# Where stores are queued and how long a side matmul waits: out-projection and up stage of a hybrid decoder layer

## The chip, the cores and the metric

One core of a Trainium2 chip runs the whole layer. The metric is the device time of one execution in microseconds (us). TensorE (PE) does the matmuls, ScalarE (ACT) and VectorE (DVE) the elementwise work, GpSimd (POOL) a few fills and many transfers, SyncE (SP) only transfers. SP, ACT and POOL each have one queue in which they start transfers (DMAs), and each of them works through its instructions in order.

## The reference, cut to what matters

x is 2048 tokens by 1024 channels, float32, one layer.

```
h   = RMSNorm(x); z = h @ w_in
mix = concat(attention(z), conv_module(z), rg_lru(z))
x   = x + mix @ w_out                       # out-projection
ff  = square(relu(RMSNorm(x) @ w_up))       # up stage, 4096 wide
x   = x + ff @ w_down                       # down stage
out = RMSNorm(x)
```

The attention is a dilated window attention with three patterns; the conv module has 31 taps, a LayerNorm (two totals over channels) and a swish; rg_lru has a 4-tap convolution, two gates by small matmuls, and a scan.

## The kernel before, in words

Channels lie on the 128 partitions and tokens along the free axis. The tokens go in two halves h of 1024. Every float32 operand is split into a rounded part and a rest (`split` L233, `halves` L887: a cast on ACT, then a subtraction on DVE), and each product is three matmuls, 128x128 by 512 columns.

The stages on PE, in order: in-projection of half 0 and of half 1, with the three mixers of half 0 beside the latter; then, for each half, out-projection, up stage, down stage. The mixers of half 1 run beside the out-projection, up and down stage of half 0.

**The mixers of half 1** are a generator, `mixers(1)`, that yields a cost after each step. The main stages call `tick(share)` (L858) at fixed places: a tick adds the share to a credit that is held under two shares, takes one step of the generator when the credit is positive, and subtracts the step's cost. A tick's PE, DVE and ACT instructions are placed behind the main ones traced so far. There are two ticks in each of the 56 groups of 24 matmuls of the down stage (L1486), seven for each of the 16 passes of the up stage and two for each out-projection tile. `yield 0` costs nothing, so it only puts the next step at the next tick. What is left of the mixers when the down stage of half 0 reaches its last product is traced at once (L1551 to L1554). The mixers of half 0 are run through without ticks, so that a yield changes nothing there. In `conv_norm` (L467) and `lru_mixer` (L522) a split is followed by a yield and then by the matmuls that read it (L275, L276; L549 to L551).

**The out-projection** (`outproj`, L993) makes 16 tiles of 128 channels by 512 tokens, tile n in the order of `ORDER` (L893): first the later 512 tokens of the half (n 0 to 7, m = 1), then the earlier (n 8 to 15, m = 0). A tile is 24 matmuls into one of four banks. Its weights, 512 KB, are loaded by `out_load` (L911) two or three tiles ahead into a buffer that an earlier tile has read, and split by `out_split`. The old x (`residual`, L1008) is loaded into `e_at`, a ring of three tiles for half 0 and of four for half 1; DVE adds the bank (L1069). `evac` (L1012) scales a copy g on ACT (L1015), stores e to `xscr` (L1016), adds the square to a sum, splits g, and makes the sums S1, S2, S3 of the 2x2 block scheme that the up stage multiplies by. It stores g to `ascr` where m = 1 (L1024), and S2 to `ascr` for tiles 8 to 11 (L1037), once two subtractions and two splits are done. These stores are POOL's, where they share the queue with the attention's loads. `in_order` (L1045) holds SP's transfers in the order in which the tile loop traces them; the other order is the scheduler's, which places instructions by when its own model has them ready.

**The up stage** (`up`, L1097) has 16 passes f of seven products with 12 matmuls each. Weights are loaded on SP (L959 to L961, L976) into buffers that the splits of the pass before free. The results are squared (L1119, L1120), summed on DVE (L1177, L1192, L1199) and stored to `fscr` by `put` (L1114), seven stores a pass on ACT's queue. The result tiles are a ring of six. The down stage (`down`, L1331) loads them again on SP.

Of the kernel before, what the change touches and what calls it, by code (L numbers as in the profile page):

```python
# [77 lines left out]
def body(tc, xt, w_in, w_v, w_out, w_up, w_down, vecs, lru_wa, lru_wx, consts, out):  # L78
    nc = tc.nc
# [50 lines left out]
    def work(h):  # L130
        return wide_tile() if h == 0 else mtile()
# [16 lines left out]
    def conv_bank():  # L148
        return pc.tile([P, NB], F32, name="cb", tag="cb")
# [17 lines left out]
    xscr = tc.dram_tile([KT, P, S], F32, name="xscr")  # L167
    nscr = tc.dram_tile([2, HS], F32, name="nscr")
    fscr = tc.dram_tile([2, 7, NSET, P, NB], F32, name="fscr")
    ascr = tc.dram_tile([3, KH, P, NB], F32, name="ascr")  # L170
# [296 lines left out]
    def conv_norm(t0, yc, early):  # L467
        tile_, q = wide_tile if early else mtile, nc.sync if early else nc.gpsimd
        s = tile_()[:, :NB]
        nc.vector.tensor_add(s, yc[0], yc[1])  # L470
        pair = work_pair(0 if early else 1)
        split(s, *pair)
        yield 1.4
        bank = conv_bank()
        total(bank, ones_cr, pair)
        yield 0
        for a in yc:
            nc.vector.tensor_sub(a, a, bank)
        q0 = tile_()[:, :NB]
        nc.scalar.activation(s, yc[0], AF.Square)  # L480
        nc.scalar.activation(q0, yc[1], AF.Square)
        yield 1.4
        nc.vector.tensor_add(q0, q0, s)
        pair = work_pair(0 if early else 1)
        split(q0, *pair)
        yield 1.4
        bank = conv_bank()
        total(bank, ones_cr, pair)
        yield 0
        nc.scalar.activation(s, bank, AF.Sqrt, bias=eps_l)  # L490
        nc.vector.reciprocal(s, s)
        yield 3.3
        for t, a in enumerate(yc):
            nc.vector.tensor_mul(a, a, s)
            nc.scalar.activation(a, a, AF.Silu, scale=v("conv_ln_g", t), bias=v("conv_ln_b", t))
        yield 1.4
        for t, a in enumerate(yc):
            q.dma_start(mscr[3 + t][:, t0:t0 + NB], a)
        yield 0
# [22 lines left out]
    def lru_mixer(h):  # L522
        n = HS if h == 0 else NB
        for t0 in range(h * HS, (h + 1) * HS, n):
            for t in range(3):
                x = work(h)
                gw = mtile_r() if h else early_gates
                loads(h).dma_start(x[:, :n + 3], lscr[t][:, t0 + 29:t0 + n + 32])
                loads(h).dma_start(gw.bitcast(F32), gates_w[t])
                u = work(h)[:, :n]  # L530
                if h:
                    yield 0
                    yield 0
                nc.vector.tensor_scalar(u, x[:, 0:n], v("lru_conv_w", t * LTAPS), v("lru_conv_b", t), op0=OP.mult, op1=OP.add)
                for k in range(1, LTAPS):
                    if k == 2:
                        yield 1.3
                    nc.vector.scalar_tensor_tensor(u, x[:, k:k + n], v("lru_conv_w", t * LTAPS + k), u, op0=OP.mult, op1=OP.add)
                yield 1.5
                r, i = work(h)[:, :n], work(h)[:, :n]  # L540
                for c in range(0, n, NB):
                    uh, ul = work_pair(h)
                    split(u[:, c:c + NB], uh, ul)
                    yield 0.7
                    for m, (dst, name) in enumerate(((r, "lru_ba"), (i, "lru_bx"))):
                        bank = mix_bank() if h and m else conv_bank()
                        wh, wl = (gw[:, part * P:(part + 1) * P] for part in (m, 2 + m))
                        with first():
                            nc.tensor.matmul(bank, wh, uh, start=True, stop=False)  # L549
                            nc.tensor.matmul(bank, wh, ul, start=False, stop=False)  # L550
                            nc.tensor.matmul(bank, wl, uh, start=False, stop=True)  # L551
                        nc.scalar.activation(dst[:, c:c + NB], bank, AF.Sigmoid, bias=v(name, t))
                    yield 0
                nc.vector.tensor_mul(u, u, i)
                gg = work(h)[:, :n]
                loads(h).dma_start(gg, gscr[t][:, t0:t0 + n])
                a = work(h)[:, :n]
                nc.scalar.activation(a, r, AF.Exp, scale=splus[:, 12 + t:13 + t])
                nc.scalar.activation(r, r, AF.Tanh, scale=splus[:, 9 + t:10 + t])
                yield 0.7  # L560
                nc.scalar.activation(i, a, AF.Square)
                nc.vector.scalar_tensor_tensor(r, i, 1.0, r, op0=OP.add, op1=OP.mult)
                nc.scalar.activation(r, r, AF.Sqrt)
                yield 0.7
                nc.vector.tensor_mul(u, u, r)
                init = 0.0 if t0 == 0 else state[:, t:t + 1]
                nc.vector.tensor_tensor_scan(i, a, u, init, OP.mult, OP.add)
                if t0 + n < S:
                    nc.vector.tensor_copy(state[:, t:t + 1], i[:, n - 1:n])
                yield 2.1  # L570
                nc.vector.tensor_mul(gg, gg, i)
                yield 0.7
                stores(h).dma_start(mscr[5 + t][:, t0:t0 + n], gg)
# [337 lines left out]
    def out_load(n, pairs):  # L911
        nc.sync.dma_start(f32(out_pair(n, pairs)[1]), out_w[ORDER[n][1]])
# [80 lines left out]
    def outproj(h, wts, banks, begun):  # L993
        at, pairs = wts.at, wts.pairs
# [17 lines left out]
        def evac(n):  # L1012
            m, d, tok = where(n)
            e, g = e_at[n % es], scaled[n % 4]
            nc.scalar.activation(g, e, AF.Copy, scale=v("norm2_g", d))  # L1015
            nc.gpsimd.dma_start(xscr[d][:, tok], e)  # L1016
            if n % 8 == 0:
                nc.scalar.activation(sq[m], e, AF.Square)
            else:
                nc.scalar.activation(sqt, e, AF.Square)  # L1020
                nc.vector.tensor_add(sq[m], sq[m], sqt)
            k = d % 4
            if m == 1:
                nc.gpsimd.dma_start(ascr[d // 4, k], g)  # L1024
            if m == 1 and d >= 4:
                split_op(A22, k, g)
                s1 = held.pop(k)
                nc.vector.tensor_add(s1, s1, g)
                split_op(S1, k, s1)
            elif m == 0 and d < 4:  # L1030
                s3, s2 = back.pop(k)
                split_op(A11, k, g)
                nc.vector.tensor_sub(s3, g, s3)
                split_op(S3, k, s3)
                nc.vector.tensor_sub(s2, s2, s3)
                split_op(S2, k, s2)
                nc.gpsimd.dma_start(ascr[2, k], s2)  # L1037
            else:
                held[k] = g

# [15 lines left out]
        for n in range(16):  # L1056
            if 1 <= n < 4:
                act_load(h, 0, *((2, 4), (4, 5), (5, 8))[n - 1])
            if n >= begun:
                out_matmuls(n, pairs, banks, range(4))  # L1060
                tick(OUT_SHARE)
                out_matmuls(n, pairs, banks, range(4, KT))
            if n + 1 < 16 and n + 1 > begun - 1:
                out_split(n + 1, pairs)
            if 1 <= n <= 4:
                act_split(0, 2 * n - 2)
                act_split(0, 2 * n - 1)
            with first():
                nc.vector.tensor_add(e_at[n % es], e_at[n % es], banks[n % 4])  # L1069
            evac(n)  # L1070
            if 4 <= n + 3 < 8:
                out_load(n + 3, pairs)
            if 8 <= n + 2 < 16:
                out_load(n + 2, pairs)
            if 7 <= n <= 10:
                back[n - 7] = s_at(), s_at()
                nc.sync.dma_start(back[n - 7][0], ascr[0, n - 7])
                nc.sync.dma_start(back[n - 7][1], ascr[1, n - 7])
            if n + 2 < 16:
                residual(n + 2)  # L1080
            if n == 12:
                wts.load(0)
            elif n == 13:
                wts.sums(0)
                wts.first()
            elif n == 14:
                wts.second()
            in_order()
            tick(OUT_SHARE)
# [7 lines left out]
    def up(h, wts, banks, rest, prologue):  # L1097
# [14 lines left out]
                nc.tensor.matmul(bank, wl[:, sl], hi(x), start=False, stop=k == KH - 1, **kw)  # L1112

        def put(q, f, t):  # L1114
            nc.scalar.dma_start(fscr[h, q, f], t)

        def squared(t, src):
            with first():
# [34 lines left out]
        for f in range(NSET + 1):  # L1153
# [8 lines left out]
            if f < NSET:  # L1162
                d = d_[f % 2]
# [357 lines left out]
    pairs = []  # L1521
# [18 lines left out]
    for h in range(2):  # L1540
        wraw, plain, at, more = low_tiles(h)
        pairs = pairs + more
# [38 lines left out]
        else:  # L1581
            pairs = state_["pairs"]
# [53 lines left out]
```

## Time and profile before

| | us |
|---|---|
| three runs | 2063.57, 2066.7, 2083.01 |
| median | 2066.7 |
| profiled execution | 2067.54 |
| its span, first to last instruction | 2065.7 |
| PE busy in the span | 1979.6 |
| DVE, ACT, POOL busy | 1500.4, 1054.6, 198.7 |

The span is what the trace covers; the execution's own time is 1.8 us longer. An engine's busy time counts its work and not the time in which it starts transfers or waits. A share of the clock below 1 in a stretch says that TensorE ran part of it at the lower of its two levels (1.2 instead of 2.4 GHz).

### The profile page before, as it was taken

The numbers are of one execution on the slowest core, as the hardware profiler recorded it, in microseconds if no ns is written. First come the engines' busy times: TensorE is split into PE (matmuls) and PEld (weight loads), VectorE is DVE, ScalarE is ACT, GpSimd is POOL, SyncE is SP. The second block draws the span as 40 slices with busy tenths as digits, with TensorE's granted clock in tenths as the row PEclk, the third lists the DMA queues.
The fourth block names the chain that finished last, engine by engine and source line by source line (L and its number), as shares of the span: only waits on it lengthen the run. The fifth ranks groups of instructions, "written<-read, shape, count | busy, mean of one in ns | idle before, by whom it ended". The sixth has DMA issues, their size and how long they took to land.

```text
span 2065.7 us, 25592 instructions
## 1 busy us (share of the span) xinstructions
PE 1979.6 (96%) x8876; PEld 1593.9 (77%) x8876; DVE 1500.4 (73%) x2009; ACT 1054.6 (51%) x1623; POOL 198.7 (10%) x352
## 2 busy tenths in 40 slices
PE   8999999999889999999999999999999999999997
PEld 6877777887667777888777778877888887778885
DVE  7898865587667665888888996777555555697855
ACT  6144974333557754465656554356455455344341
POOL 0113100000233413000000000120000000000000
PEclk9999999999999999999999999999999999999999
DMA  5555684734786648445976684685444448876834
GB/s 172 171 147 156 181 293 145 254 118 134 227 249 174 199 141 252 151 169 183 357 264 237 207 286 157 216 280 192 152 153 149 151 149 290 307 264 215 271 106 143
DMA packets 205165, 416.31 MB, mean 202 GB/s; under 512 B 26118, under 2 KB 34550, under 8 KB 204972
## 3 DMA queue, kind: packets, MB, share of 16 engines
q1 hardware_dynamic: 148884, 284.86, 42.1%
q0 software_dynamic: 20688, 60.59, 9.5%
q10 hardware_dynamic: 35464, 69.23, 9.0%
q8 instruction: 70, 1.15, 0.2%
q14 instruction: 59, 0.48, 0.1%
HBM read 299.79 MB, written 123.19 MB: 205 GB/s over the span
## 4 chain that ended last, share of the span: by engine, by line
PE 66%; DMA 12%; DVE 11%; issue 6%; ACT 4%; POOL 1%; SPq 1%; DVEq 0%; ACTq 0%; POOLq 0%
PE bank L1110 9%; PE bank L1111 9%; PE bank L1112 9%; PE bank L1425 6%; PE bank L1424 6%; PE bank L1426 6%; DMA rounded<-fscr 4%; PE mm L255 3%; PE mm L258 3%; PE mm L261 3%; DMA pair<-out_w 3%; DVE rounded L889 2%; DVE wide L462 2%; PE bank L926 1%; PE bank L924 1%
## 5 line engine op out<-in xcount | busy, mean ns | idle before, releaser
L1110 PE MATMUL bank<-rounded,pair 128*128 128x512 f32 x896 | 355.2, 396 | 3.5 <-ACT low L1208 3.0
L1111 PE MATMUL bank<-rounded,pair 128*128 128x512 f32 x896 | 353.0, 394 | 0.0
L1112 PE MATMUL bank<-rounded,pair 128*128 128x512 f32 x896 | 352.0, 393 | 0.0
L888 ACT CAST rounded<-rounded 128x1024 fp32r<-128x1024 f32 (+1 forms) x168 | 160.3, 967 | 310.2 <-DMA rounded<-fscr 220.8
L889 DVE TENSOR_TENSOR rounded<-rounded 128x1024 fp32r<-128x1024 f32 (+1 forms) x168 | 185.9, 1117 | 130.3 <-ACT rounded L888 130.1
L1425 PE MATMUL bank<-rounded,rounded 128*128 128x512 f32 x672 | 263.5, 392 | 7.0 <-DVE rounded L889 7.0
L1424 PE MATMUL bank<-rounded,rounded 128*128 128x512 f32 x672 | 263.9, 393 | 5.5 <-DVE z L1437 3.8
L1426 PE MATMUL bank<-rounded,rounded 128*128 128x512 f32 x672 | 262.7, 391 | 0.0
L1110 PEld LDWEIGHTS bank<-rounded,pair 128*128 128x128 f32 x896 | 168.6, 188 | 44.2 <-ACT low L1208 3.4
L1112 PEld LDWEIGHTS bank<-rounded,pair 128*128 128x128 f32 x896 | 168.7, 188 | 37.2 <-issue 0.4
L1111 PEld LDWEIGHTS bank<-rounded,pair 128*128 128x128 f32 x896 | 168.8, 188 | 35.9 <-issue 0.5
L255 PE MATMUL mm<-rounded,rounded 128*128 128x512 f32 x496 | 160.1, 399 | 9.3 <-ACT rounded L235 7.6
L261 PE MATMUL mm<-rounded,rounded 128*128 128x512 f32 x496 | 158.5, 394 | 0.0
L258 PE MATMUL mm<-rounded,rounded 128*128 128x512 f32 x496 | 158.0, 396 | 0.0
L1424 PEld LDWEIGHTS bank<-rounded,rounded 128*128 128x128 f32 x672 | 126.7, 189 | 36.5 <-issue 5.8
L1425 PEld LDWEIGHTS bank<-rounded,rounded 128*128 128x128 f32 x672 | 126.6, 188 | 36.1 <-DVE rounded L889 9.7
L1426 PEld LDWEIGHTS bank<-rounded,rounded 128*128 128x128 f32 x672 | 126.7, 189 | 26.4
L235 ACT CAST rounded<-raw 128x512 fp32r<-128x512 f32 (+1 forms) x96 | 55.7, 583 | 158.8 <-PE mm L258 105.3
L888 ACT CAST pair<-wraw 128x1024 fp32r<-128x1024 f32 x64 | 67.2, 1051 | 115.0 <-PE bank L1111 85.9
L889 DVE TENSOR_TENSOR rounded<-block,rounded 128x1024 fp32r<-128x1024 f32 x96 | 116.3, 1217 | 6.3 <-ACT rounded L888 6.3
L889 DVE TENSOR_TENSOR pair<-wraw,pair 128x1024 fp32r<-128x1024 f32 x64 | 78.2, 1221 | 58.6 <-ACT pair L888 58.6
L255 PEld LDWEIGHTS mm<-rounded,rounded 128*128 128x128 f32 x496 | 93.4, 190 | 31.5 <-ACT rounded L235 7.9
(325 smaller groups left out, 3816.7 us busy)
## 6 DMA issues: line engine op xcount, KB each, us to landing
block<-in_w_down SPq DMA_DIRECT2D x128, 512.0 KB, 5.4
fscr<-low ACTq DMA_DIRECT2D x224, 256.0 KB, 2.1
rounded<-fscr SPq DMA_DIRECT2D x112, 512.0 KB, 4.9
raw<-in_w_in SPq DMA_DIRECT2D x64, 256.0 KB, 3.8
wraw<-in_w_up SPq DMA_DIRECT2D x64, 256.0 KB, 3.0
low<-in_w_up SPq DMA_DIRECT2D x64, 256.0 KB, 3.2
pair<-out_w SPq DMA_DIRECT2D x24, 512.0 KB, 5.7
raw<-in_xt SPq DMA_DIRECT2D x32, 256.0 KB, 3.6
```

The lines of the kernel that those rows point to most:

```text
L235: nc.scalar.copy(h, raw)
L255: nc.tensor.matmul(bank, wh[:, sl], ah[:, cols], start=first_, stop=False)
L258: nc.tensor.matmul(bank, wh[:, sl], al[:, cols], start=False, stop=False)
L261: nc.tensor.matmul(bank, wl[:, sl], ah[:, cols], start=False, stop=last_)
L888: nc.scalar.copy(h, raw)
L889: nc.vector.tensor_sub(l, raw, f32(h))
L1110: nc.tensor.matmul(bank, wh[:, sl], hi(x), start=fresh and k == 0, stop=False, **kw)
L1111: nc.tensor.matmul(bank, wh[:, sl], lo(x), start=False, stop=False, **kw)
L1112: nc.tensor.matmul(bank, wl[:, sl], hi(x), start=False, stop=k == KH - 1, **kw)
L1424: nc.tensor.matmul(banks[j], th[:, c], sh[:, x], start=fresh and k0, stop=False, **kw)
L1425: nc.tensor.matmul(banks[j], th[:, c], sl[:, x], start=False, stop=False, **kw)
L1426: nc.tensor.matmul(banks[j], tl[:, c], sh[:, x], start=False, stop=k1, **kw)
```

## The change

One `yield 0` is added behind three splits, so that the matmuls that read the split come one tick later. The stores to `xscr` and `ascr` in `evac` go from POOL's queue to SP's, and the weight load of tiles 8 to 15 is traced ahead of `evac` instead of behind it. All stores of `put` go from ACT's queue to SP's.

```diff
@@ conv_norm (twice)
         split(s, *pair)
         yield 1.4
+        yield 0
         bank = conv_bank()
         total(bank, ones_cr, pair)
@@ lru_mixer
                     split(u[:, c:c + NB], uh, ul)
                     yield 0.7
+                    yield 0
@@ outproj, evac
-            nc.gpsimd.dma_start(xscr[d][:, tok], e)
+            nc.sync.dma_start(xscr[d][:, tok], e)
...
-                nc.gpsimd.dma_start(ascr[d // 4, k], g)
+                nc.sync.dma_start(ascr[d // 4, k], g)
...
-                nc.gpsimd.dma_start(ascr[2, k], s2)
+                nc.sync.dma_start(ascr[2, k], s2)
@@ outproj, tile loop
                 nc.vector.tensor_add(e_at[n % es], e_at[n % es], banks[n % 4])
+            if 8 <= n + 2 < 16:
+                out_load(n + 2, pairs)
             evac(n)
             if 4 <= n + 3 < 8:
                 out_load(n + 3, pairs)
-            if 8 <= n + 2 < 16:
-                out_load(n + 2, pairs)
@@ up
         def put(q, f, t):
-            nc.scalar.dma_start(fscr[h, q, f], t)
+            nc.sync.dma_start(fscr[h, q, f], t)
```

## Rows read from the trace of the kernel before

**Rows 1.** The page: span, busy time of the engines, shares of the chain that ended last.
```profile
span 2065.7 us, 25592 instructions
PE 1979.6 (96%) x8876; PEld 1593.9 (77%) x8876; DVE 1500.4 (73%) x2009; ACT 1054.6 (51%) x1623; POOL 198.7 (10%) x352
...
PE 66%; DMA 12%; DVE 11%; issue 6%; ACT 4%; POOL 1%; SPq 1%; DVEq 0%; ACTq 0%; POOLq 0%
```
**Rows 2.** Windows (header names the columns): out-projection 0, down 0, up 1.
```profile
500.00:640.00 140.00, 123.43 (x584) 96.04 (x583) 90.90 (x171) 80.08 (x152) 43.00 (x74) 0.94 0.73 223
970.00:1240.00 270.00, 252.52 (x1069) 202.01 (x1068) 240.52 (x246) 157.84 (x184) 12.85 (x24) 0.98 0.79 273
1430.00:1745.00 315.00, 315.00 (x1370) 256.63 (x1369) 179.03 (x230) 165.96 (x251) 0.00 (x0) 1.00 0.47 164
```
**Rows 3.** Windows: three stretches of 10 us in which the clock fell.
```profile
core 0: us, PE busy (x) PEld busy (x) DVE busy (x) ACT busy (x) POOL busy (x), PEclk, DMA share, GB/s
530.00:540.00 10.00, 7.11 (x28) 5.26 (x29) 4.67 (x10) 7.50 (x15) 0.54 (x1) 0.66 0.69 239
800.00:810.00 10.00, 8.61 (x32) 6.97 (x32) 3.72 (x6) 6.25 (x10) 2.16 (x4) 0.83 0.98 314
1090.00:1100.00 10.00, 6.25 (x21) 4.30 (x20) 8.63 (x10) 8.93 (x12) 0.00 (x0) 0.83 0.81 293
```
**Rows 4.** Waits of PE: who was waited for, us in all, times, longest.
```profile
PE mb L730 <- ACT m L718: 10.1, 8, 5.0
PE cb L549 <- ACT mr L235: 6.7, 4, 3.4
PE bank L1110 <- ACT low L1208: 3.0, 1, 3.0
PE cb L275 <- ACT mr L235: 2.6, 1, 2.6
```
**Rows 5.** Timeline of the last tail of the mixers, then of product 5's evacuation (DVE).
```profile
1205.80 0.69 DVE L571 TENSOR_TENSOR m<-m 128x512 f32<-128x512 f32 x1
...
1237.29 1.27 DVE L1437 TENSOR_TENSOR z<-z,bank 128x512 f32<-128x512 f32 x2
```
**Rows 6.** Lines L1016 and L1115: ns of an issue, min/median/max, first and last start.
```profile
L1016 POOL DMA_DIRECT2D xscr<-low x16: 540/552/598, 514.9 to 636.8; - x16
...
L1115 ACTq DMA_DIRECT2D fscr<-low x224: 325/326/644, 660.3 to 1743.4; - x112
```
**Rows 7.** Timeline of SP and ACT, out-projection 0.
```profile
520.28 0.33 SPq L1010 DMA_DIRECT2D low<-in_xt  x1
...
521.19 0.38 SPq L912 DMA_DIRECT2D pair<-out_w  x1
...
529.36 1.04 ACT L888 CAST pair<-pair 128x1024 fp32r<-128x1024 f32 x1 [2.70 <-DMA pair<-out_w]
```
**Rows 8.** Waits of SP's queue.
```profile
SPq L1010 <- DMA xscr<-low: 63.4, 11, 9.7
```
**Rows 9.** DMA issues: KB each, median us to landing.
```profile
fscr<-low ACTq DMA_DIRECT2D x224, 256.0 KB, 2.1
...
pair<-out_w SPq DMA_DIRECT2D x24, 512.0 KB, 5.7
...
xscr<-low POOLq DMA_DIRECT2D x16, 256.0 KB, 5.2
```
**Rows 10.** Timeline of out-projection 1: S2 of tile 9, load 12, start of tile 13.
```profile
1390.05 0.38 SPq L912 DMA_DIRECT2D pair<-out_w  x1
...
1393.26 0.68 DVE L1035 TENSOR_TENSOR wraw<-wraw 128x512 f32<-128x512 f32 x1
...
1406.06 0.50 PE L924 MATMUL bank<-rounded,pair 128*128 128x512 f32 x1 [2.63 <-ACT pair L888]
```
**Rows 11.** Timeline of DVE and ACT, up stage of half 0.
```profile
794.45 0.69 DVE L979 TENSOR_TENSOR low<-low,wraw 128x512 f32<-128x512 f32 x1 [5.66 <-DMA low<-in_w_up]
...
795.78 3.99 ACTq L1115 DMA_DIRECT2D fscr<-low  x4
...
799.81 1.05 ACT L888 CAST pair<-wraw 128x1024 fp32r<-128x1024 f32 x1 [8.28 <-DVE low L1199]
```

More of the change, by code (lines that the diff above doesn't have):

```diff
@@ L544, in lru_mixer @@
                     yield 0.7
+                    yield 0
                     for m, (dst, name) in enumerate(((r, "lru_ba"), (i, "lru_bx"))):
```

## The prediction

> **What bounds the kernel now.** The page first: PE is busy for 1979.6 of the 2065.7 us of the span, and two thirds of the chain that ended last are PE's own matmuls [rows 1]. So a change can only give back PE's idle 86 us and whatever the lower clock level costs. The windows by stage then say where such time lies. The up stage of half 1 has none: 315 of 315 us busy at the full clock, 1370 matmuls, 0.230 us each. The first out-projection is busy for 123.4 of 140 us at a granted clock of 0.94, and the down stage beside the mixers for 252.5 of 270 at 0.98 [rows 2]. The short windows show that the two losses belong together: after a stall PE runs on for some us at 1.2 instead of 2.4 GHz, and the share of the clock that is missing is lost as well, 3.4 us of the ten after the longest stall [rows 3]. PE's waits name the causes: an attention transpose that waits for the exponentials on ACT (10.1 us, one of them 5.0), the gate matmuls of the LRU that wait for the cast of their operand (6.7), the LayerNorm total (2.6), and one product of the up stage held by a copy on ACT (3.0) [rows 4].
>
> **Part 1, the extra tick.** It applies to four totals and six gate steps of half 1. A tick of the down stage is half of 24 matmuls, 12 x 0.230 = 2.8 us [rows 2]. The waits that it is aimed at are 6.7 + 2.6 = 9.3 us, the longest 3.4 [rows 4], so that a delay of 2.8 covers all but some 0.6 us. After two of them the clock fell, as in the window from 1090, where 0.17 of ten us is missing [rows 3]; 1.7 us each, 3.4 in all. The most is then 12 us. It adds no instruction, only place: what is late next is DVE, busy for 240.5 of the 270 us [rows 2], and I expect it to take some of this back. I take 9; the ends are 0 (each wait moves to the next tick or to DVE) and 12. The price is at the end: ten ticks of 2.8 put the mixers' last step 28 us later, from 1205.8 to 1234, and the drain comes with the last product, just behind the additions at 1237 [rows 5]. It fits by one tick. If it does not, one scan and one multiplication are traced in a lump, and their mixer output is read tens of us later: 0 to 3 us.
>
> **Part 2, stores of the out-projections to SP.** POOL loses 16 + 8 + 4 issues in each half, 56 of 0.54 us [rows 6]; SP gets them at 0.33 to 0.38 [rows 7], about 20 us spread over 250. That is nothing by itself, since SP does nothing but start transfers; what counts is who waits behind what.
>
> What goes: SP's load of the old x waits for an e tile whose store POOL has still to send, 63.4 us over 11 waits [rows 8], and the weight load behind it comes late. At 520.28 SP gets its tile; the weights of tile 5 are issued at 521.19 and reach their cast at 529.36 [rows 7]. ACT stands before that cast, and the exponentials that PE's transpose needs stand behind it: this is the 5.0 us wait, and the clock of 0.66 follows it. With the store on SP, it is issued when the addition is done, one tile before the ring needs it, and POOL's attention loads no longer stand behind the stores. The scheduler orders ACT anew too.
>
> What comes: each weight load now stands behind the stores of the tile before, thus behind DVE's addition and ACT's copy of that tile. For tiles 4 to 10 that is about 1.5 us after the tile's last matmul (addition and copy; an addition of that size takes 0.68 [rows 10], and I take the copy to be the same). The weights need 5.7 us to land [rows 9] and 1.04 to be cast [rows 7]; two tiles, 11 us, lie between. That fits with 3 us to spare, and not when a load takes 8 us as the one at 521. For tiles 11 to 14 the load stands behind S2. In the second projection S2 of tile 9 is done at 1393.9, and four issues (its store, two loads of ascr, one of x) lie between it and the load of tile 12: 1395.4, where before it was 1390.05. Landed and cast that is 1402.1. Tile 13 started at 1406.06 after a stall of 2.63 [rows 10], so tile 12 began at 1406.06 - 2.63 - 24 x 0.230 = 1397.9. I get a stall of 4.2 us in each projection, once: it also delays the two tiles behind, whose loads depend on tiles ahead of it, so that at most every third tile can stall. The ends are 0 and two stalls, 8.4 us each.
>
> The sum of this part. The first projection has 140 - 123.4 = 16.6 us of idle PE and 0.06 x 140 = 8.4 of clock [rows 2]. I expect the long stalls and most of the clock to go, 18 of 25, then 4 us of new stall in each projection: 10 us net. The ends are +25 and a loss that the rivals price.
>
> **Would landing be faster on another queue?** By the rows, stores of 256 KB land 5.2 us after POOL's issue, in the crowded projection, and 2.1 after ACT's, in the quiet up stage [rows 9]; the load differs as much as the queue, so I count nothing for it. The Trainium skill (DMA: Bandwidth & Descriptors, section Issuing engines are not separate DMA queues) says that transfers of all issuing engines end on the same 16 DMA engines, and that the choice of issuer saves only the time of starting them, usually small. By that rule parts 2 and 3 would be worth nothing, and the sum 2067.5 - 9 = 2058, near the first rival below. No row here compares the queues under equal load; the rule leaves out the wait in the issuer's own order, which is the term that I count.
>
> **Part 3, stores of the up stage to SP.** 224 issues of 0.33 us leave ACT [rows 6]. In the steady passes PE has no idle time [rows 2], so nothing can be won there. Once it can: at 794.45 DVE had waited 5.66 us for weights; the four stores in ACT's queue wait for DVE's sums, and the cast behind them starts at 799.81 after 8.28 us of idle ACT [rows 11]. PE lost 3.0 us there [rows 4] and then 0.17 of ten us of clock [rows 3]. With the stores elsewhere ACT passes on: 4.7 us, of which I take 4. The cost is on SP, where a store now stands between weight loads. Each is ready within the same pass (84 x 0.230 = 19.3 us) as before and takes 0.33, and in its model the scheduler sorts them by readiness; seven more issues are 2.3 us of a pass. I count 0. The cover is the lead of the weights; where it fails, a store that waits for a sum holds a load, at most the 8.28 us seen on ACT, once or twice: 0 to 12 us.
>
> **The sum.** 9 + 10 + 4 = 23 us off the profiled execution's 2067.5 (span 2065.7 and 1.8 around it), which is 0.8 above the median: 2044.5, rounded to 2044.
>
> **Rivals.** *The DMA engines bound the projections.* They are busy for 0.73 of the first projection's time [rows 2], weights that take 8 us hold ACT whoever sends the stores, and the stalls only change place. Then parts 2 and 3 give back 4 us at most and part 1 its 9: 2067.5 - 13 = 2054. For it: the load issued at 521.19 had left SP one us after the tile that held it, and spent eight on the way [rows 7]. Against it: 63.4 us of SP's waits are for one named store. *One load at a time.* A store of tile n waits for ACT's copy g, and the load of later weights stands behind that store. If ACT has the cast of weights still on the way ahead of the copy, each load starts only when the one before has landed: 5.7 to land, 1.04 cast, 0.7 copy, 0.4 issue, 7.8 us a tile against 24 x 0.230 = 5.5. Eight loads stand behind a store of g; 8 x 2.3 less the 3 us of lead is 15, and 3.4 of clock, 19 a projection; the stalls of before stay, and parts 1 and 3 give 13: 2067.5 + 38 - 13 = 2092, slower. It decides by ACT's order: by whether the scheduler's model has the weights landed before the tile's addition. For it: ACT stood 2.7 us before such a cast [rows 7]. Against it: that cast was placed for a load that stood behind no store; placed anew it should come later. *The tick is not the limit.* ACT's cast is late because of casts ahead of it that wait for DMAs, and one more tick finds the next of them; the projections gain what they lose. Then nothing moves: 2067.
>
> **Chances.** My forecast 0.52 (2030 to 2058), DMA-bound 0.20 (2048 to 2060), nothing 0.13 (2060 to 2072), one load at a time 0.15 (2070 to 2100). 1% of the median, about what a measurement of this kernel can tell from no change, is 20.7 us: 2046.0 and 2087.4 are the bounds. Of my own case six tenths lie below 2046, of the DMA-bound one two tenths: 0.31 + 0.04 = 0.35 for faster; of the last case two thirds lie above 2087: 0.10 for slower; 0.55 between. Leaving out half of the slower case and the far end of the best gives 2028 to 2075.
>
> **What would show it.** Part 1: the waits of L549 and L275 for the cast on ACT are gone (under 2 us), and the mixers' last step lies between 1210 (if the time before it shrinks as forecast) and 1235. Part 2: SP's wait for xscr at L1010 is near 0, the window of the first projection has a clock of 0.97 or more and 8 us less idle PE; in the second there is one stall of about 4 us near tile 12. Part 3: no gap of ACT above 5 us in the up stage of half 0, and PE at 100% in the second up stage as before. It is wrong if PE waits for the cast of out-projection weights (L888) several times in each projection, or if idle PE appears between 1430 and 1745.

## Result and profile after the change

The changed kernel takes 2054.9 us (median; 2044.7 to 2064.9), the kernel before, beside it on the same chip, 2072.8. The ratio is 0.9909, with a 95% interval of 0.9887 to 0.9931: 0.9% faster, some 19 us, where 23 were forecast. The profiled execution took 2052.3 us, 1.8 of them around a span of 2050.4. Lines above the edits keep their numbers; below the third tick each is three higher (L1010 is now L1013, L912 L915, L549 L552).

The page after: span, PE's busy time, shares of the chain.

```profile
span 2050.4 us, 25667 instructions
...
PE 1974.6 (96%) x8876; PEld 1588.8 (77%) x8876; DVE 1501.0 (73%) x2009; ACT 1054.1 (51%) x1623; POOL 167.9 (8%) x296
...
PE 58%; issue 15%; DMA 13%; DVE 9%; ACT 4%; SPq 1%; POOL 1%; DVEq 0%; ACTq 0%; POOLq 0%
```

PE does the same 8876 matmuls [rows 1]; POOL has 56 instructions fewer. The windows after, with the columns of [rows 2]:

```profile
500.00:640.00 140.00, 133.08 (x654) 102.02 (x652) 103.75 (x193) 89.10 (x170) 28.09 (x46) 1.00 0.77 240
970.00:1240.00 270.00, 254.83 (x1092) 205.13 (x1091) 239.56 (x241) 153.96 (x176) 12.85 (x24) 0.99 0.77 263
1430.00:1745.00 315.00, 313.65 (x1366) 256.18 (x1365) 178.21 (x224) 164.47 (x242) 0.00 (x0) 1.00 0.49 171
```

The first out-projection has 9.65 us more of busy PE in the same 140, and its granted clock rose from 0.94 to 1.00. The last window still covers the second up stage, but also the first us of the down stage behind it, since everything lies earlier; the idle 1.35 us stand in that part, at 1716.9 and after.

The short windows, as in [rows 3], and a new one at 1110:

```profile
530.00:540.00 10.00, 10.00 (x50) 7.88 (x49) 8.69 (x16) 7.40 (x16) 4.04 (x7) 1.00 0.99 287
800.00:810.00 10.00, 10.00 (x45) 8.15 (x44) 8.61 (x12) 6.29 (x10) 0.00 (x0) 1.00 0.73 266
1090.00:1100.00 10.00, 10.00 (x46) 8.28 (x45) 10.00 (x12) 9.82 (x12) 0.00 (x0) 1.00 0.41 128
1110.00:1120.00 10.00, 4.79 (x13) 3.49 (x12) 6.07 (x8) 4.53 (x6) 0.00 (x0) 0.69 0.60 227
```

PE is busy at the full clock in all three old windows. The first and the third stall are gone; of the second a wait of 1.7 us is left, which now lies ahead of its window, at 798. One new stall stands at 1110. PE's waits after name both:

```profile
PE mb L733 <- ACT m L721: 5.6, 6, 2.1
PE bank L1427 <- ACT v L1435: 5.5, 2, 5.2
...
PE cb L552 <- ACT mr L235: 1.7, 2, 1.1
PE bank L1113 <- ACT low L1193: 1.7, 1, 1.7
```

The longest waits of [rows 4] have become short ones, and the 5.2 us for which a bank waits for ACT's copy v in the down stage are new (before, this copy cost PE 0.7 us).

A balance by stage, worked out from the traces: idle PE (the gaps in front of matmuls that start in the stage) + half of the time that the records show at half clock, in us. A stage runs from its first product to that of the next, and a stretch at half clock counts where it starts. One profile each; the times of the kernel before spread over 19 us from run to run, so differences of 2 or 3 us in one cell carry nothing.

| kernel | in-proj. and before | out-proj. 0 | up 0 | down 0 | out-proj. 1 | up 1 | down 1 |
|---|---|---|---|---|---|---|---|
| before | 22.0 + 1.7 | 16.1 + 8.5 | 7.6 + 3.4 | 14.9 + 3.4 | 5.0 + 1.7 | 0 + 0 | 6.6 + 5.4 |
| whole change | 21.0 + 3.4 | 6.3 + 0 | 2.4 + 0 | 16.2 + 3.4 | 8.6 + 0 | 0.3 + 0 | 7.5 + 8.5 |
| part 1 alone | 18.8 + 1.7 | 15.5 + 8.5 | 4.0 + 3.4 | 19.3 + 6.8 | 5.9 + 3.4 | 0 + 0 | 7.5 + 10.2 |
| part 2 alone | 21.2 + 5.1 | 6.0 + 0 | 6.7 + 1.7 | 16.4 + 5.1 | 8.2 + 0 | 0.3 + 0 | 7.8 + 7.0 |
| part 3 alone | 21.1 + 1.7 | 16.5 + 8.5 | 4.2 + 0 | 11.8 + 1.7 | 6.5 + 3.4 | 0 + 0 | 5.0 + 7.0 |
| parts 2 and 3 | 20.7 + 3.4 | 5.5 + 0 | 4.9 + 0 | 11.5 + 3.4 | 6.6 + 3.4 | 0.2 + 0 | 7.5 + 6.6 |
| 2 and 3, load not moved | 21.5 + 3.4 | 15.3 + 11.9 | 5.7 + 1.7 | 10.8 + 1.7 | 17.1 + 5.1 | 1.2 + 0 | 3.9 + 5.6 |

By this balance the whole change wins 18 us in the first out-projection and 9 in the first up stage, and nothing in the down stage at which the tick was aimed. The balance overstates the first: a wait during half clock counts twice (1.8 us there before), and short waits are not seen whole, since the ends of matmuls are modelled. So the lengths of the stages, from the starts of matmuls, are given beside it. The first projection, first to last product, fell from 126.4 to 111.9 us with the same 532 matmuls in it, 14.5 less; the first up stage fell from 352.3 to 343.6; the down stage behind it has 339.6 after 339.0; the second projection grew from 97.1 to 101.9 (two matmuls of the up stage lie in it now).

### The profile page after: what moved, and what is told of

It reads as the page before. It is cut to its first block, busy times and chain, and to the rows that moved or that the text cites. A ratio compares the mean times of both kernels' runs of the same rounds, so it can differ in the third digit from the quotient of the medians.

```text
span 2050.4 us, 25667 instructions
## 1 busy us (share of the span) xinstructions
PE 1974.6 (96%) x8876; PEld 1588.8 (77%) x8876; DVE 1501.0 (73%) x2009; ACT 1054.1 (51%) x1623; POOL 167.9 (8%) x296
## 4 chain that ended last, share of the span: by engine, by line
PE 58%; issue 15%; DMA 13%; DVE 9%; ACT 4%; SPq 1%; POOL 1%; DVEq 0%; ACTq 0%; POOLq 0%
PE bank L1113 9%; PE bank L1114 9%; PE bank L1115 9%; PE bank L1428 4%; PE bank L1429 4%; PE bank L1427 4%; DMA rounded<-fscr 4%; PE mm L255 4%; PE mm L261 4%; PE mm L258 4%; DMA pair<-out_w 2%; DVE rounded L892 2%; DVE wide L462 1%; DMA m<-oscr 1%; DMA wraw<-in_w_up 1%
## 5 line engine op out<-in xcount | busy, mean ns | idle before, releaser
L1115 PE MATMUL bank<-rounded,pair 128*128 128x512 f32 x896 | 351.0, 392 | 0.0
L1428 PE MATMUL bank<-rounded,rounded 128*128 128x512 f32 x672 | 264.2, 393 | 5.3 <-DVE rounded L892 5.3
L1115 PEld LDWEIGHTS bank<-rounded,pair 128*128 128x128 f32 x896 | 168.4, 188 | 37.4 <-issue 0.6
L1428 PEld LDWEIGHTS bank<-rounded,rounded 128*128 128x128 f32 x672 | 127.2, 189 | 34.6 <-DVE rounded L892 8.0
```

The lines of the kernel that those rows point to most:

```text
L1428: nc.tensor.matmul(banks[j], th[:, c], sl[:, x], start=False, stop=False, **kw)
```

## Experiments

Each ratio is to the kernel before, measured beside it on the same chip, with its 95% interval. The runs come from three chips; kernels of different chips are compared by these ratios alone.

### The three parts, each alone

**Part 1: the ticks.** Twice in the conv norms (`yield 1.4`), once in the LRU (`yield 0.7`):

```diff
         yield 1.4
+        yield 0
         bank = conv_bank()
...
                     yield 0.7
+                    yield 0
                     for m, (dst, name) in ...
```

> The kernel before with the extra tick alone. My theory (the matmuls read a split that ACT makes a little too late, and one tick of 2.8 us covers it): PE's waits of L549 and L275 for ACT's cast fall from 9.3 us to under 3 and the ratio to the kernel before is 0.995 to 0.998, up to 9 us less. Rival (ACT's cast is late because of what stands before it, one tick finds the next of it): the waits move to other lines of the down stage, ratio 0.999 to 1.001.

Measured: 2065.4 us, 0.9986 (0.9970 to 1.0002), not told apart from no change; the forecast of 9 us off (0.9956) lies outside the interval. PE's waits from 970 to 1330 in this kernel:

```profile
PE bank L1428 <- DVE rounded L892: 6.8, 6, 2.0
PE bank L1427 <- ACT v L1435: 3.7, 1, 3.7
...
PE cb L552 <- ACT mr L235: 1.6, 1, 1.6
```

The wait of the gate matmuls fell from 6.7 us [rows 4] to 1.6 and that of the total to nothing, so the tick does what it says. But L1425's wait for DVE, the same line before the shift as L1428 here, was 5.2 us in that window and is 6.8, and the 3.7 for the copy v were 0.7. The balance: down 0 from 14.9 to 19.3 us of idle PE. By length down 0 went from 339.0 to 346.0 us and up 0, at whose end the wait of the total lay, from 352.3 to 349.6. This profile is of the slowest of twelve executions (2073.4 us).

**Part 2: stores of the out-projections, and the load that moves with them.**

```diff
-            nc.gpsimd.dma_start(xscr[d][:, tok], e)
+            nc.sync.dma_start(xscr[d][:, tok], e)
...   (the two ascr stores likewise)
+            if 8 <= n + 2 < 16:
+                out_load(n + 2, pairs)
             evac(n)
             if 4 <= n + 3 < 8:
                 out_load(n + 3, pairs)
-            if 8 <= n + 2 < 16:
-                out_load(n + 2, pairs)
```

> The kernel before with the out-projections' stores on SP and the earlier weight load, no more. Theory (SP's load of the old x waited for a store that stood in POOL's queue, and the weights behind it were late): the first projection's window has some 18 us less of idle PE and lost clock, the second some 4 more, ratio 0.992 to 0.996. Rival (the DMA engines bound the projection): weights land as late as before, the first projection keeps its 16.6 us of idle PE, ratio 0.998 to 1.002.

Measured: 2060.1 us, 0.9961 (0.9949 to 0.9973). Out-projection 0 gains what the whole change gains there (6.0 + 0 against 6.3 + 0), and out-projection 1 has 3.2 us more idle PE.

**Part 3: stores of the up stage.**

```diff
-            nc.scalar.dma_start(fscr[h, q, f], t)
+            nc.sync.dma_start(fscr[h, q, f], t)
```

> The kernel before with the up stage's stores on SP and no more. Theory: one gap of ACT before the cast of weights in the first up stage goes (3 us of PE and 1.7 of clock), nothing else moves, ratio 0.997 to 0.999. Rival (stores that wait for sums hold back SP's weight loads): PE gets idle time in the up stages, ratio 1.001 to 1.006.

Measured: 2058.2 us, 0.9958 (0.9942 to 0.9974), 9 us where 4 were forecast. Window of this kernel for down 0:

```profile
970.00:1240.00 270.00, 257.21 (x1104) 206.57 (x1103) 243.03 (x248) 161.41 (x186) 12.89 (x24) 0.99 0.80 277
```

The gap in up 0 shrank as forecast (the balance: 7.6 + 3.4 to 4.2 + 0). Down 0 has 4.7 us more busy PE than in [rows 2], though part 3 moves nothing of that stage; the order of the instructions on PE and ACT differs from up 0 on. This is no scatter of one profile: seven kernels of this document have the stores of half 0 on SP and no added tick, and their down 0 takes 332.6 to 335.5 us; the five without the tick whose stores stay on ACT or go to POOL take 339.0 to 342.3.

The product of the three ratios is 0.9905, the whole change has 0.9909: the parts add up.

**Does the tick pay beside the others?** Parts 2 and 3 without part 1:

> Parts 2 and 3 together, without the extra tick. Theory (the parts add up and the tick is worth next to nothing): the ratio to the kernel before is the product of the two parts measured alone, 0.9961 x 0.9958 = 0.992, some 2052 to 2054 us where before takes 2069, and no clearer than that from the whole change (0.991). Rival (the tick pays once the stalls elsewhere are gone): 0.9955 or more, and the gate matmuls L549 and the total L275 wait for the cast on ACT for 6 us or more, against 1.7 in the whole change.

Measured: 2046.5 us against 2064.9, 0.9913 (0.9886 to 0.9940). That is the ratio of the whole change: the tick adds nothing that can be measured. The two intervals together are some 7 us wide to either side, so that the 9 forecast would have shown. The lengths say why: down 0 takes 334.7 us here and 339.6 with the tick, up 0 347.3 and 343.6, as in part 1 alone. PE's wait of this kernel for the cast of the gates' operand:

```profile
PE cb L549 <- ACT mr L235: 3.1, 2, 2.0
```

With 1.7 us for the total, half of the 9.3 us that the tick was aimed at went without it; the rival's 6 or more did not come.

### Why the out-projection gains

**A fourth e tile, on the kernel before.** The load of the old x waits for the store of an e tile; one more tile takes the wait away and leaves the queue as it was.

```diff
-            e_at, scaled = at[5:7] + at[15:16], at[8:12]
+            e_at, scaled = at[5:8] + at[15:16], at[8:12]
```

> The kernel before with four instead of three tiles in the ring e_at of half 0, stores still on POOL. It takes away what SP's load of the old x waits for, without moving a store. Theory (that wait delays the weights): SP's 63 us of waits for xscr fall under 25, the first projection's idle PE falls by 5 to 15 us, ratio 0.993 to 0.998. Rival (the gain comes from POOL's queue being freed for the attention's loads, or from nothing but the order of the scheduler): SP's waits fall, PE's idle time in the first projection stays, ratio 0.999 to 1.002.

Measured: 2062.2 us, 0.9974 (0.9961 to 0.9988). SP's wait for these stores and the first out-projection in this kernel:

```profile
SPq L1010 <- DMA xscr<-low: 15.6, 6, 7.7
```

```profile
500.00:640.00 140.00, 127.32 (x621) 98.94 (x621) 95.27 (x180) 84.22 (x161) 45.40 (x77) 0.98 0.76 233
```

The wait fell from 63.4 us [rows 8] to 15.6, and two thirds of part 2's gain (0.9974 against 0.9961) came with it. So the wait is a cause, not a bystander. The projection takes 115.8 us, first to last product, 10.6 less than before; part 2 alone has 111.4. (This profile, too, is of the slowest of twelve executions, 2068.3 us.) The first long stall shows how: the load of tile 5 leaves SP at 518.97, not at 521.19 [rows 7], and ACT's cast of it, here at 524.09, waits 1.10 us and not 2.70; the exponentials run behind it at 526.97, and PE's wait for them is 0.38 us, not 5.0.

**The stores on ACT's queue.** Part 2 with `nc.scalar` in place of `nc.sync` in its three stores, the load moved:

> Part 2 with ACT's queue in place of SP's, the weight load moved as in part 2. Theory (the 63.4 us of SP's waits go because the store no longer stands in POOL's queue; ACT has just made the copy of the tile, so the store leaves at once): SP's wait for xscr under 15 us, clock of the first projection 0.97 or more, and a ratio of 0.996 as with SP. Rival (ACT bounds the projection; 56 issues of some 0.4 us and S2's store, which waits for DVE, hold its casts): the clock stays at 0.94 to 0.96 and the ratio is 0.999 or more.

Measured: 2066.5 us, 1.0010 (0.9994 to 1.0025). Window, SP's wait, and landing (KB each, median us) in this kernel:

```profile
500.00:640.00 140.00, 129.38 (x627) 101.28 (x626) 95.39 (x179) 83.92 (x157) 25.70 (x42) 0.98 0.76 234
```

```profile
SPq L1010 <- DMA xscr<-low: 53.4, 9, 7.8
```

```profile
xscr<-low ACTq DMA_DIRECT2D x16, 256.0 KB, 5.9
```

The theory failed: leaving POOL takes only 10 of the 63 us from SP's wait; the store lands after 5.9 us here and after 5.2 from POOL [rows 9]. The first out-projection gains all the same (PE busy 129.4, clock 0.98; 117.8 us long, 8.6 less than before), though less than on SP (111.4), and the time is not better. Some of the loss lies elsewhere: the projection begins at 513.4 us, where it began at 508.1, and no store was moved ahead of it. Why is open. Where the first stall went, ACT's timeline of this kernel shows:

```profile
530.60 0.51 ACT L718 ACTIVATE m<-m,ncol 128x256 f32<-128x256 f32 x1
...
535.07 1.05 ACT L888 CAST pair<-pair 128x1024 fp32r<-128x1024 f32 x1
```

The exponentials now stand ahead of the first cast of weights in this stretch, and no wait of PE is left there.

**Only the x stores on SP.** Parts 2 and 3 without the tick, but both ascr stores on POOL's queue, as before:

```diff
-                nc.sync.dma_start(ascr[d // 4, k], g)
+                nc.gpsimd.dma_start(ascr[d // 4, k], g)
...
-                nc.sync.dma_start(ascr[2, k], s2)
+                nc.gpsimd.dma_start(ascr[2, k], s2)
```

> Parts 2 and 3 without the extra tick, only the sixteen xscr stores of a half on SP; the ascr stores (g and S2) stay on POOL. Theory (the one wait that counted was that of the old x for the xscr store; the other stores only stand in front of weight loads): ratio 0.987 to 0.990, first projection at clock 0.98 or more. Rival (the g and S2 stores also come late from POOL, and the loads of ascr that read them back hold SP): 0.992 to 0.995.

Measured: 2057.2 us against 2066.8, 0.9956 (0.9938 to 0.9973). The theory (0.987 to 0.990) fails, and the ratio is a little above the rival's as well (0.992 to 0.995): the ascr stores count too. SP's queue in this kernel:

```profile
SPq L1091 <- DMA ascr<-wraw: 14.2, 2, 7.2
```

L1091 loads S2 back. With its store on POOL, SP stands 14.2 us at that load for the store to land, and the weight loads stand behind it.

**Only S2's store on POOL** (the second pair of lines of that diff):

> Parts 2 and 3 without the extra tick, S2's store (four in a half) left on POOL's queue. Theory (the new waits for weights in the second projection come from loads behind S2's store on SP): idle PE there falls from 6.6 to 3 us or less, ratio 0.989 to 0.990 against 0.9913. Rival (S2's store costs SP nothing that counts, the new waits come from elsewhere): 0.991 to 0.992.

Measured: 2053.1 us, 0.9930 (0.9908 to 0.9952). The gain that the theory expected did not come: idle PE in out-projection 1 is 10.2 us, not 3 or less, and SP's wait at L1091 is 13.2. The second projection is 107.5 us long, first to last product, against 102.7 with S2's store on SP. Against 0.9913 the time can't tell same from worse, nor 0.9930 from the 0.9956 of the run before; so what each ascr store is worth is not shown by the times.

**Four e tiles on top:**

> Parts 2 and 3 without the extra tick, and four e tiles in half 0 instead of three. Theory (with the store on SP nothing waits for it any more, so the fourth tile has nothing left to cover): ratio 0.991 to 0.992, as without it. Rival (the load of the old x still stands behind DVE's addition of the tile before, and one more tile gives it lead): first projection 2 to 5 us shorter, 0.989 to 0.990.

Measured: 2054.6 us, 0.9945 (0.9926 to 0.9965). The fourth tile has nothing left to cover: out-projection 0 has 7.3 + 1.7, against 5.5 + 0 without it. Against 0.9913 the time can't tell same from worse.

### The load that moves with the stores

Parts 2 and 3 without the tick, the load of tiles 8 to 15 left behind `evac(n)`:

```diff
-            if 8 <= n + 2 < 16:
-                out_load(n + 2, pairs)
             evac(n)
             if 4 <= n + 3 < 8:
                 out_load(n + 3, pairs)
+            if 8 <= n + 2 < 16:
+                out_load(n + 2, pairs)
```

> Parts 2 and 3 without the extra tick, and with the weight loads of tiles 8 to 15 left behind the stores of the tile before, as in the kernel before. Theory (a load behind a store that waits for ACT's copy g and for DVE's S2 starts late): idle PE of the second projection 4 to 15 us more than the 6.6 with the loads moved, the same again in the first, ratio 0.996 to 1.003 against 0.9913. Rival (the tile's stores leave at once, the loads have the lead): 0.991 to 0.993.

Measured: 2083.3 us against 2066.8, 1.0079 (1.0055 to 1.0103), **slower** than before and 1.7% above the same kernel with the load moved (0.9913). The first out-projection, and PE's and ACT's waits in the whole of this kernel:

```profile
500.00:640.00 140.00, 124.69 (x558) 93.96 (x556) 86.25 (x160) 76.02 (x142) 21.56 (x36) 0.91 0.65 212
```

```profile
ACT pair L888 <- DMA pair<-out_w: 37.2, 15, 6.9
...
PE bank L924 <- ACT pair L888: 21.8, 9, 3.9
```

The timeline of one tile of out-projection 1 in it:

```profile
1374.64 0.32 SPq L1016 DMA_DIRECT2D xscr<-m  x1
...
1376.21 0.32 SPq L912 DMA_DIRECT2D pair<-out_w  x1
...
1382.56 0.32 SPq L1016 DMA_DIRECT2D xscr<-m  x1
...
1384.77 0.32 SPq L1037 DMA_DIRECT2D ascr<-wraw  x1
1385.14 0.42 SPq L912 DMA_DIRECT2D pair<-out_w  x1
...
1390.37 0.50 PE L924 MATMUL bank<-rounded,pair 128*128 128x512 f32 x1 [2.99 <-ACT pair L888]
```

A load is issued behind the stores of its own step: 1.6 us after the addition's store, 2.6 where S2 stands between. One tile of matmuls, 5.5 us, is left to land (4.1 us median here) and to be cast and subtracted (1.04 and 1.23). That doesn't fit, and PE waits: each projection has 10 us more idle PE than with the load moved, and the clock costs 12 and 2 more in the balance, 34 us in all, as the ratios say. The theory had the mechanism and expected less (0.996 to 1.003).

### Where part 3's gain comes from

**Half 0 alone:**

```diff
-            nc.scalar.dma_start(fscr[h, q, f], t)
+            (nc.scalar if h else nc.sync).dma_start(fscr[h, q, f], t)
```

> Part 3 for half 0 alone; the stores of the up stage of half 1 stay on ACT. Theory (the second up stage has no idle PE to give back): the whole gain of part 3 stays, ratio 0.996, and the gap in the first up stage is 1.8 us or less with no fall of the clock behind it. Rival (the freed ACT helps in both halves, through later casts): half of the gain, 0.998.

Measured: 2060.8 us, 0.9976 (0.9961 to 0.9990). Between the two theories, and too near to both to decide: some half or more of part 3's gain is from half 0. What half 1 adds (0.9958 / 0.9976 = 0.9982) is within the two intervals' widths and stays open; the second up stage itself takes 310.6 us in both kernels, and 310.8 before.

**POOL's queue in place of SP's** (`nc.gpsimd` in that line):

> Part 3 with POOL's queue in place of SP's. Theory (what counts is that ACT no longer waits behind stores for DVE's sums): ratio 0.996 as with SP. First rival (SP's order by readiness is what counts): 1.000. Second rival (POOL's attention loads of half 1, behind the stores, come late): PE idle in the first up stage grows from 4 to over 10 us, ratio 1.003 or more.

Measured: 2065.3 us, 0.9996 (0.9979 to 1.0013). ACT is as free as in part 3, and PE's gap before 800 is gone (its longest between 690 and 970 is 0.46 us), but the gain is not there. POOL's longest wait in the first up stage of this kernel:

```profile
POOL fscr L1115 <- ACT low L1120: 90.2, 26, 15.0
```

The stores now hold POOL, whose attention loads and stores stand behind them: PE loses 2.1 and 1.6 us in attention at 642 and 683 (before, 1.3 and nothing), up 0 has 10.0 us of idle PE and down 0 17.5. Of the 10.0, 3.3 are the total's wait at the end of the stage, which was 2.6 before. That comes near the first half of the second rival (over 10 us in up 0), without its price (1.003 or more). A free ACT alone gave nothing here: what the stores' new queue holds up counts as well.

## Why the prediction was right, and which of its steps were not

The forecast (2044, 1.1% under the median shown; range 2028 to 2075) had the direction, and the parts add up as it summed them: 23 us forecast, 19 measured. Of the 11 us by which the measured 2054.9 lies above 2044, 6 are the kernel before, whose median beside it was 2072.8 and not 2066.7. Of its three terms one was nearly right by a wrong reading, one too large and one too small: that the sum came within 4 us is in part luck, since the errors of parts 1 and 3 cancel.

**Part 1 failed.** Forecast 9 us, measured 3 alone (0 to 6) and nothing beside the other parts. The two signs that it named came: L552's wait is under 2 us, L275's is gone, and the mixers' last step lies at 1213.5, between 1210 and 1235:

```profile
1213.50 0.68 DVE L574 TENSOR_TENSOR m<-m 128x512 f32<-128x512 f32 x1
```

The price was read well: the last step comes 248.8 us after the first product of down 0, before 218.7, so 30 us later where 28 were forecast. What failed is the step "I expect it to take some of this back": nearly all of it was taken back, and not by DVE alone. In part 1's window PE waits 5 us more for DVE (12.6 against 7.4) and 4 us more for ACT's copy v and casts of weights (5.1 against 0.7), where 7.7 went. The first half of the rival "the tick is not the limit" described it: ACT's casts wait in order for a DMA, and PE finds the next of them. The timeline of the new stall, after:

```profile
1107.49 0.37 SPq L1264 DMA_DIRECT2D rounded<-fscr  x1
...
1114.18 1.04 ACT L891 CAST rounded<-rounded 128x1024 fp32r<-128x1024 f32 x1 [5.33 <-DMA rounded<-fscr]
1115.13 1.06 ACT L1435 COPY v<-bank 128x512 f32<-128x512 f32 x2
...
1115.77 0.79 PE L1427 MATMUL bank<-rounded,rounded 128*128 128x512 f32 x1 [5.21 <-ACT v L1435]
```

ACT stands 5.3 us at a cast whose operand SP asked for at 1107.49; the copies that free PE's banks stand behind it, and 3.4 us of clock follow. Part 1 alone has the like (3.7 us); in none of the twelve kernels without the tick does PE wait for this copy for more than 1.1 us in all. With the tick down 0 is longer in both pairs, by 7.0 us alone and by 4.9 beside parts 2 and 3.

**Part 2: the sum held, the reading of the wait did not.** Forecast 10 us, measured 8; by length the first projection gives back 14.5 us and the second costs 4.8, net 9.7. The prediction said that SP waits for a store "that POOL has still to send". The trace of before says otherwise; the addition and the store of the tile for which SP waited until 526.84:

```profile
519.59 0.69 DVE L1069 TENSOR_TENSOR low<-low,bank 128x512 f32<-128x512 f32 x1
...
520.57 0.57 POOL L1016 DMA_DIRECT2D xscr<-low  x1 [3.70 <-DVE low L1069]
```

POOL sent it 0.29 us after the addition was done. What SP's load at 526.84 waited for was its landing, six us later (5.2 in the median [rows 9]). So it is with all: the 16 stores of that projection leave POOL 0.3 to 0.9 us after their additions. After the change the loads of x no longer wait, but SP itself stands at the x stores of both halves until the addition is done:

```profile
SPq L1019 <- DVE m L1072: 40.7, 14, 10.9
SPq L1019 <- DVE low L1072: 37.5, 11, 5.5
```

So the sign that SP's wait for xscr is near 0 came, and yet SP starts the weight loads no earlier: that of tile 5 leaves at 528.23, where it left at 521.19. For tiles 4 to 15 of the first projection a load left 10 to 26 us ahead of its tile's first matmul before, and leaves 8 to 13 ahead after; in the second it was 7 to 18 and is 7 to 9, which is the price there. What is better in the first is the landing of this load, with the stores' own (KB each, median us to landing, after),

```profile
xscr<-low SPq DMA_DIRECT2D x16, 256.0 KB, 3.2
```

and above all ACT's order. Before, the cast of tile 5's weights stood ahead of the exponentials, at 529.36 [rows 7], some 17 us before PE came to tile 5 (its first matmul is at 546.18). After:

```profile
524.93 0.51 ACT L721 ACTIVATE m<-m,ncol 128x256 f32<-128x256 f32 x1
...
532.70 1.05 ACT L891 CAST pair<-pair 128x1024 fp32r<-128x1024 f32 x1 [1.10 <-DMA pair<-out_w]
```

The load is later, the cast stands later with it, and the exponentials run first. The prediction had this in one sentence ("the scheduler orders ACT anew too") and counted nothing for it. For this stall three kernels agree: a load 2.2 us earlier cures it (the fourth e tile), and so does a cast behind the exponentials, with the stores on SP's queue (the whole change) or on ACT's. The longest wait of the projection before, 5.1 us for a copy on ACT (L733), has the same form; ACT's timeline before:

```profile
604.85 1.05 ACT L888 CAST pair<-pair 128x1024 fp32r<-128x1024 f32 x1 [5.01 <-DMA pair<-out_w]
...
611.17 0.57 ACT L733 COPY m<-mb 128x512 f32<-128x512 f32 x1
```

The third long one, 3.6 us for DVE (L708), was not followed. How the whole gain of the first projection divides between the two causes is open.

The new cost was placed exactly and the one stall sized too large. Forecast: 4.2 us before tile 12 of out-projection 1, whose load stands behind S2 of tile 9. The timeline after, to be read beside [rows 10]:

```profile
1371.58 0.68 DVE L1038 TENSOR_TENSOR wraw<-wraw 128x512 f32<-128x512 f32 x1
1372.29 0.32 SPq L1040 DMA_DIRECT2D ascr<-wraw  x1
...
1374.14 0.38 SPq L915 DMA_DIRECT2D pair<-out_w  x1
...
1381.18 0.50 PE L927 MATMUL bank<-rounded,pair 128*128 128x512 f32 x1 [2.44 <-ACT pair L891]
```

S2 is done at 1372.26; its store, two loads of ascr and one of x follow; the load of tile 12 leaves at 1374.14, 1.9 us after S2 (1.5 forecast), and PE waits 2.44 us, then 0.53 for the subtraction. "Once" was not right: PE waits for weights before five other tiles too, where before the change it waited before three, so that the stage has 3.6 us more idle PE than before (its clock loss of 1.7 is gone) and is 4.8 us longer. In the first projection the stall forecast for it did not appear. Its net gain of 14.5 us by length fits the forecast of 18 less 4 all the same, which is luck: the 18 was counted as the balance counts, which shows 18.3 where the projection is 14.5 us shorter, and the 4 did not come.

**Part 3 was right in its place and too small.** The gap of 8.28 us on ACT [rows 11] is gone; ACT's casts there, after:

```profile
796.64 1.03 ACT L891 CAST pair<-wraw 128x1024 fp32r<-128x1024 f32 x1
...
801.03 1.05 ACT L891 CAST pair<-wraw 128x1024 fp32r<-128x1024 f32 x1 [2.88 <-PE bank L1114]
```

PE's gap there is 1.70 us, where it was 2.97, and the clock does not fall: 1.3 + 1.7 = 3 of the 4 forecast. The other 6 of the 9 us measured are in no term: the prediction looked for the gain in the up stages alone and had nothing for the stage behind them. In the profile of part 3 alone, down 0 has 4.8 us less loss and is 5.5 us shorter (333.5 against 339.0), and with the stores of half 0 alone 3.5 (335.5). No store of that stage moved; ACT's and PE's order from up 0 on differs. That is where it shows, not why; the cause stays open. The cover named, the lead of the weights on SP, held: PE has no idle time in the second up stage.

**The slower rival.** "One load at a time" priced a projection at 19 us, if each load waits for the stores of the tile before it to get through ACT. It did not happen, and the kernel with the load not moved shows how near it was: 34 us above its twin (0.0166 of 2067), 17 a projection, PE waiting for the casts. There, too, it is the load's place behind a store that decides. The prediction's answer, that a cast placed anew would come later on ACT, came true for tile 5, but it does not keep the projections from getting slower; what does is the line that moves `out_load(n + 2)` ahead of `evac(n)`: two tiles of matmuls, not one, lie between the load's issue and its use, as the prediction's own lead of 11 us had it (8 to 13 measured in the first projection, 7 to 9 in the second). It did not say that the same stores without that line would be slower.

**DMA-bound projections** did not happen: the DMA share of the first projection's window rose from 0.73 [rows 2] to 0.77, and its granted clock to 1.00. The prediction set beside that rival a rule of the Trainium skill (DMA: Bandwidth & Descriptors, section Issuing engines are not separate DMA queues): starting transfers on several engines saves only the time of starting them. By it, parts 2 and 3 would be worth nothing; measured, part 2 is 0.9961 on SP and 1.0010 on ACT, and part 3 0.9958 on SP and 0.9996 on POOL. That the transfers share engines is not contradicted; what the sentence leaves out is the order in which an issuer waits.

## What to carry to other kernels

When a store is moved to the queue that also loads, look first at which load then stands behind it and how much work is left until that load is used: here the place of one weight load decided between 0.9913 and 1.0079. A queue's wait for a store may be for its landing, not its sending: here all 16 stores had left within 0.9 us of their producer, so compare the two before blaming the sender's queue. A weight load that leaves later can even help, when its cast then stands behind the work that PE needs first. And a wait met with one more tick of other work may only change its name: here PE next waited for copies on ACT that stood behind a cast waiting for a DMA, so add up all waits of the stage, not the one aimed at.

## What the runs showed of the hardware

The same 256 KB store of x in the first out-projection landed after 5.2 us (median) from POOL's queue [rows 9], 5.9 from ACT's and 3.2 from SP's. The weights of 512 KB, all issued by SP in that window, took 5.8 us before, 8.2 with the stores on ACT, and 4.8 after. These medians rest on few landings, since a trace does not show all: 16 of the 16 stores from POOL, 7 from ACT and 8 from SP, and 6, 3 and 4 of the weight loads. And the order of the three queues does not hold elsewhere. In the second projection the store took 3.8 us from POOL, 3.7 from ACT and 3.8 from SP (KB each, median us to landing; POOL's line is of before, SP's of after):

```profile
xscr<-m POOLq DMA_DIRECT2D x16, 256.0 KB, 3.8
xscr<-m SPq DMA_DIRECT2D x16, 256.0 KB, 3.8
```

In the up stages the stores to `fscr` took 2.1 us from ACT, 2.2 from SP and 2.9 from POOL. So what else is on the way counts for at least as much as the queue; that SP's queue makes a store land sooner is not shown. A store that shares SP's queue with the loads is sent only when SP gets to it, and SP stands at it until its producer is done: 40.7 and 37.5 us in all at the x stores after the change.
